# Layer-one norm weights applied to the activations, and weight segments split in halves of 1024 columns

## The chip, the cores and the metric

One core of one Trainium2 chip runs the whole program. The metric is device time in microseconds (us) of one launch. Engines are named as in the profile: PE is TensorE's matmuls and PEld its weight loads, DVE is VectorE, ACT is ScalarE, POOL is GpSimd, SP the queue that issues most transfers.

## The reference, cut to what matters

The input is 512 tokens by 1024 features, all float32. Layer one is a Mamba-2 mixer, layer two a differential attention. Only layer one is touched:

```python
h = rms_norm(x, norm_g)                      # x * rsqrt(mean(x*x) + eps) * norm_g
zxbcdt = h @ w_in                            # 1024 -> 2048 (z) + 4096 (x, B, C) + 32 (dt)
...                                          # conv, SiLU, chunked state-space scan -> y
u = y * silu(z);  u = group_rms_norm(u)      # 8 groups of 256
x = x + (u * gate_norm_g) @ w_out            # 2048 -> 1024
```

`norm_g` has one weight for each row of `w_in`, and `gate_norm_g` one for each row of `w_out`. So each may multiply the rows of the weights or the features of the activation: the product is the same.

## The kernel before, in words

**Three matmuls for one.** Every float32 operand of a big product is cut into two: `hi`, its rounding to the type fp32r, and `lo`, the remainder. `mm3` then adds three matmuls: hi by hi, and the two mixed ones. Making the pair costs one ACT instruction (the rounding copy into `hi`) and one DVE instruction (`lo` = operand minus `hi`).

**Segments.** Layer one's weights come in 32 segments of 1 MB, each a tile `raw` of 128 partitions by 4 blocks (k) of 512 columns: 8 for z, 16 for the eight groups' B, C and x, 8 for the out projection. `order_a` is their order. A segment feeds 16 calls of `mm3`, 48 matmuls. `load` issues the transfer and returns `split`, which gives four pieces, one for each k; a piece is `head` (ACT, `raw` to `whi`) and `rest` (DVE, `raw` and `whi` to `wlo`). With `gains`, both multiply by a norm weight held per partition in `prm`, while they split. `raw`, `whi` and `wlo` have two buffers each: the split of a segment waits until the matmuls of the segment two before it are through, its transfer until the split of the segment two before it is done.

**Who fixes the order.** TensorE's order is the written order (`T.on`). `TURNS` interleaves a segment's blocks for some projections. On DVE and ACT the planner orders layer one's instructions, from priorities and its own estimate of durations; `fetch` lays the pieces of a segment down at high priority. The state-space work of a group (`ssd`) is put between the dense matmuls at the places in `PLACES`. Only the first segment's pieces, which alternate with `split_x`, are in written order on DVE and ACT.

**The places that the change touches.** `split_x` splits the transposed input into `a_hi` and `a_lo` (tiles of `hh`, `hl`), unscaled. At the end of `ssd`, a group's output is transposed into PSUM (`pyt`) and split into `yh` and `yl`, unscaled. `source` hands out the norm weights. Around them: `z_out` (SiLU of a z block, `zs`, frees a PSUM bank), `conv` (a multiplication by `r_row` and three taps on DVE, tile `xc`, frees a PSUM bank); four banks (`mm`) serve the dense products in turn. The dt projection takes its own scaled weights and the raw input.

Of the kernel before, what the change touches and what calls it, by code (L numbers as in the profile page):

```python
# [9 lines left out]
F32 = mybir.dt.float32  # L10
F32R = mybir.dt.float32r
I32 = mybir.dt.int32
AF = mybir.ActivationFunctionType
ALU = mybir.AluOpType
# [42 lines left out]
C_GA, C_GK, C_GB, C_GG, C_SG, C_DTB, C_AL, C_CB, C_CW = 0, 8, 16, 24, 40, 41, 42, 43, 75  # L57
# [24 lines left out]
def trunk(ctx, tc, x, x_t, par, w_dt, w_in, w_out, w_kvqg, w_bo, d_skip, lam_qk, fin_g, out):  # L82
    nc = tc.nc
    V, A, T = (Ordered(tc, e) for e in (nc.vector, nc.scalar, nc.tensor))
# [14 lines left out]
    def ss_bank(name):  # L99
        turns[0] += 1  # L100
        tag = "mm" if turns[0] % turns[1] >= 3 else "ss"
        return psum.tile([P, 512], F32, tag=tag, name=name, bufs=3 if tag == "ss" else 4)
# [8 lines left out]
    segs = []  # L111
# [4 lines left out]
    prm = const.tile([P, C_CB], F32, name="prm")  # L116
# [8 lines left out]
    def source(seg):  # L125
        kind, a, b = seg
        if kind == "z":
            return w_in[a * 6 + b], [prm[:, C_GA + 4 * b + i:C_GA + 4 * b + i + 1] for i in range(4)]
        if kind == "g":
            return w_in[(a // 2) * 6 + 2 + (a % 2) * 2 + b], [prm[:, C_GA + 4 * b + i:C_GA + 4 * b + i + 1] for i in range(4)]  # L130
        if kind == "o":
            return w_out[a * 2 + b], [prm[:, C_GG + 4 * a + i:C_GG + 4 * a + i + 1] for i in range(4)]
        if kind in "bc":
            return w_bo[a], None
        name = f"v{a}" if kind == "v" else a
        at = C_GK if kind in "vk" else C_GB
        ks = range(4 * b, 4 * b + 4) if kind == "v" else range(8)
        return w_kvqg[BLOCKS.index((name, b))], [prm[:, at + i:at + i + 1] for i in ks]
# [5 lines left out]
    def load(i):  # L144

        seg = segs[i]
        src, gains = source(seg)
        nk = 8 if seg[0] in "kqt" else 4
        w = 2048 // nk
        raw = begun[i] if i in begun else wp.tile([P, nk, w], F32, tag="raw", name=f"raw{i}", bufs=2)  # L150
        fetched[0] += 1

        def split():

            pool, tags = (bp, ("dec", "dec")) if seg == ("o", 3, 1) else (wp, ("whi", "wlo"))
            if pool is bp:
                hi, lo = (pool.tile([P, N_DEC], F32R, tag=tag, name=f"{n}{i}", bufs=2)[:, 0:2048].rearrange("p (k n) -> p k n", k=nk)
                          for n, tag in zip(("whi", "wlo"), tags))
            else:
                hi, lo = (pool.tile([P, nk, w], F32R, tag=tag, name=f"{n}{i}", bufs=2) for n, tag in zip(("whi", "wlo"), tags))  # L160
            ready[seg] = (hi, lo)

            def head(k):
                if gains:
                    A.activation(hi[:, k, :], raw[:, k, :], AF.Copy, scale=gains[k])
                else:
                    A.copy(hi[:, k, :], raw[:, k, :])

            def rest(k):
                if gains:  # L170
                    V.scalar_tensor_tensor(out=lo[:, k, :], in0=raw[:, k, :], scalar=gains[k],
                                           in1=hi[:, k, :].bitcast(F32), op0=ALU.mult, op1=ALU.subtract)
                else:
                    V.tensor_tensor(out=lo[:, k, :], in0=raw[:, k, :], in1=hi[:, k, :].bitcast(F32), op=ALU.subtract)

            return [(head, rest, k) for k in range(nk)]

        if i == 0:

            nc.sync.dma_start(raw[:, 0, :], src[:, 0:w])  # L180
            for n in range(2):
                nc.sync.dma_start(xt[0][:, 0, n * 256:(n + 1) * 256], x_t[:, 0, n * 256:(n + 1) * 256])
            nc.sync.dma_start(raw[:, 1, :], src[:, w:2 * w])
            for n in range(2):
                nc.sync.dma_start(xt[0][:, 1, n * 256:(n + 1) * 256], x_t[:, 1, n * 256:(n + 1) * 256])
            for k in range(2, 4):
                nc.sync.dma_start(raw[:, k, :], src[:, k * w:(k + 1) * w])
                nc.sync.dma_start(xt[1][:, k - 2, :], x_t[:, k, :])

            nxt, (src1, _) = wp.tile([P, nk, w], F32, tag="raw", name="raw1", bufs=2), source(segs[1])  # L190
            begun[1] = nxt
            for i in range(2, 4):
                nc.sync.dma_start(xt[i], x_t[:, 2 * i:2 * i + 2, :])
                nc.sync.dma_start(nxt[:, 2 * i - 4:2 * i - 2, :].rearrange("p k n -> p (k n)"), src1[:, (2 * i - 4) * w:(2 * i - 2) * w])
            nc.sync.dma_start(prc[:], par[:, C_CB:N_PAR])
        elif i not in begun:
            nc.sync.dma_start(raw.rearrange("p k n -> p (k n)"), src)
        return split
# [94 lines left out]
    def root1(ss, vb, k, tag):  # L293

        s, y, c, nv = (small.tile([P, 1], F32, tag=f"{tag}_{i}", name=f"{tag}_{i}", bufs=2) for i in "sycn")
        A.activation(s, ss, AF.Sqrt, scale=k, bias=vb)

        def rest():
            V.tensor_scalar(out=nv, in0=ss, scalar1=-k, scalar2=vb, op0=ALU.mult, op1=ALU.subtract)
            V.reciprocal(y, s)  # L300
            V.tensor_scalar(out=c, in0=y, scalar1=nv, scalar2=y, op0=ALU.mult, op1=ALU.mult)
            V.tensor_scalar(out=y, in0=c, scalar1=3.0, scalar2=y, op0=ALU.add, op1=ALU.mult)
            return y

        return rest
# [55 lines left out]
    def new_h(tag):  # L361
        return [res.tile([P, KD, S], F32R, tag=f"hT_{i}", name=f"{tag}_{i}") for i in ("hi", "lo")]
# [9 lines left out]
    hh, hl = new_h("a")  # L372
# [24 lines left out]
    xt = [bp2.tile([P, 2, S], F32, tag="yl", name=f"xt{i}", bufs=4) for i in range(4)]  # L397

    def split_x(k, n=slice(0, S)):
        A.copy(hh[:, k, n], xt[k // 2][:, k % 2, n])  # L400
        V.tensor_tensor(out=hl[:, k, n], in0=xt[k // 2][:, k % 2, n], in1=hh[:, k, n].bitcast(F32), op=ALU.subtract)


    begin = small.tile([P, 1], F32, name="begin", bufs=1)
# [5 lines left out]
    for k in range(4):  # L410
        lay(first[k])
        for n in (slice(0, 256), slice(256, S)) if k < 2 else (slice(0, S),):
            split_x(k, n)
# [5 lines left out]
    for k in range(4, KD):  # L419
        split_x(k)  # L420
# [202 lines left out]
    def ssd(g):  # L623
# [7 lines left out]
        for c in range(NQ):  # L631
            cs = slice(c * P, (c + 1) * P)
# [10 lines left out]
        for j in range(2):  # L643
# [6 lines left out]
            with tc.issue_after(next_b.ins) if next_b else ExitStack():  # L650
                V.tensor_tensor(out=xdt[:, :, 2 * j:2 * j + 2, :], in0=pv, in1=dt_tok[:, :, h2].unsqueeze(3).to_broadcast([P, NQ, 2, HD]), op=ALU.mult)
                V.tensor_tensor(out=dx[:, :, 2 * j:2 * j + 2, :], in0=pv,
                                in1=dsk[:, h2].unsqueeze(1).unsqueeze(3).to_broadcast([P, NQ, 2, HD]), op=ALU.mult)
# [24 lines left out]
        for q in (1, 0):  # L678
            for c in (2 * q, 2 * q + 1):
                for h in reversed(range(R)):  # L680
                    o = (c % 2) * 256 + h * HD
# [14 lines left out]
        for c in (2, 3):  # L696
            T.matmul(po2[:, (c - 2) * 256:(c - 1) * 256], lhsT=cc[:, c * P:(c + 1) * P], rhs=hsf[:, c - 1], start=True, stop=True)
        V.tensor_tensor(out=tmp[:, 1], in0=po1[:, 256:512].rearrange("p (h e) -> p h e", e=HD),
                        in1=eacs_tok[:, 1, hs].unsqueeze(2).to_broadcast([P, R, HD]), op=ALU.mult)
        V.tensor_tensor(out=tmp[:, 2:4], in0=po2.rearrange("p (c h e) -> p c h e", h=R, e=HD),  # L700
                        in1=eacs_tok[:, 2:4, hs].unsqueeze(3).to_broadcast([P, 2, R, HD]), op=ALU.mult)
# [15 lines left out]
        yh = bp2.tile([P, 2, S], F32R, tag="yh", name=f"yh{g}", bufs=4)  # L717
        yl = bp2.tile([P, 2, S], F32R, tag="yl", name=f"yl{g}", bufs=4)
        pyt = [ss_bank(f"pyt{g}_{j}") for j in range(2)]

        n = 2 if g == G - 1 else NQ
        for j, a in [(j, a) for a in range(0, NQ, n) for j in range(2)]:
            if not j:
                yield f"y{a}"
            for c in range(a, a + n):
                T.transpose(pyt[j][:, c * P:(c + 1) * P], tm[:, c, j * P:(j + 1) * P], ident)
            cs = slice(a * P, (a + n) * P)
            A.copy(yh[:, j, cs], pyt[j][:, cs])
            V.tensor_tensor(out=yl[:, j, cs], in0=pyt[j][:, cs], in1=yh[:, j, cs].bitcast(F32), op=ALU.subtract)
        yT[g] = (yh, yl)  # L730

    T.on = True
# [4 lines left out]
    hh, hl = new_h("b")  # L737
# [284 lines left out]
    def half(t, n):  # L1022
        hs = slice(n * 512, (n + 1) * 512)
        return x_tok[:, t, hs], fg[:, hs], ot[t][:, hs], out[t * P:(t + 1) * P, hs]
# [99 lines left out]
    rest = root1(st[h][8][:, 3:4], vb, 4.0 / P, "o1")  # L1124
# [23 lines left out]
    y, f, o, dst = half(3, 0)  # L1148
# [8 lines left out]
    y, f, o, dst = half(3, 1)  # L1157
# [68 lines left out]
```

## Time and profile before

| | |
|---|---|
| time, three runs | median 708.38 us (708.01 to 709.41) |
| profiled execution | 709.16 us, span 707.4 us |
| PE, PEld | busy 697.1 us (99%), 579.8 us (82%) |
| DVE, ACT, POOL | busy 519.5 us (73%), 426.2 us (60%), 113.4 us (16%) |
| transfers | 70.85 MB, mean 100 GB/s |
| costliest group of DVE | `wlo` from `raw`, `prm`, `whi`: 240 instructions, 148.7 us |
| costliest group of ACT | `whi` from `raw`, `prm`: 240 instructions, 133.6 us |

The span runs from the first to the last instruction; what the profiled execution took beyond it lies around the program. Layer one fills about 0 to 410 us, layer two the rest. Nearly every DVE, ACT and PE instruction is recorded under line 73, a helper, so groups are told apart by tile names: `pz`, `pg`, `po` are the PSUM tiles of the z, group and out projections.

### The profile page before, as it was taken

The numbers are of one execution on the slowest core, as the hardware profiler recorded it, in microseconds if no ns is written. First come the engines' busy times: TensorE is split into PE (matmuls) and PEld (weight loads), VectorE is DVE, ScalarE is ACT, GpSimd is POOL, SyncE is SP. The second block draws the span as 40 slices with busy tenths as digits, with TensorE's granted clock in tenths as the row PEclk, the third lists the DMA queues.
The fourth block names the chain that finished last, engine by engine and source line by source line (L and its number), as shares of the span: only waits on it lengthen the run. The fifth ranks groups of instructions, "written<-read, shape, count | busy, mean of one in ns | idle before, by whom it ended". The sixth has DMA issues, their size and how long they took to land.

```text
span 707.4 us, 10489 instructions
## 1 busy us (share of the span) xinstructions
PE 697.1 (99%) x3838; PEld 579.8 (82%) x3838; DVE 519.5 (73%) x1181; ACT 426.2 (60%) x931; POOL 113.4 (16%) x158
## 2 busy tenths in 40 slices
PE   8999999999999999999999999999999999999996
PEld 7787888887788888888888888888888888888884
DVE  5479975888579669568996846457778657788786
ACT  6748673664653636637636357567777567765556
POOL 0008422402406025041110101000000000000002
PEclk9999999999999999999999999999999999999999
DMA  8643313233033331331122311313112221113003
GB/s 296 253 151 152 120 59 149 91 120 120 38 142 120 100 137 62 111 128 60 60 76 105 120 60 49 136 62 113 67 60 79 86 75 61 68 56 116 31 1 119
DMA packets 13492, 70.85 MB, mean 100 GB/s; under 512 B 1793, under 2 KB 3329, under 8 KB 6017
## 3 DMA queue, kind: packets, MB, share of 16 engines
q1 hardware_dynamic: 13008, 69.90, 27.0%
q8 instruction: 30, 0.49, 0.3%
q10 hardware_dynamic: 432, 0.28, 0.1%
q14 instruction: 22, 0.17, 0.1%
HBM read 68.02 MB, written 2.16 MB: 99 GB/s over the span
## 4 chain that ended last, share of the span: by engine, by line
PE 88%; DVE 4%; DMA 3%; ACT 2%; issue 1%; POOL 1%; SPq 0%; ACTq 0%; POOLq 0%
PE pg L73 23%; PE po L73 16%; PE pt L73 8%; PE pz L73 7%; PE pq L73 6%; PE pk L73 6%; PE pv L73 6%; PE pb L73 3%; DMA raw<-in_w_in 3%; PE sc L73 3%; PE pyd L73 2%; PE pc L73 2%; DVE wlo L73 1%; PE pcb L73 1%; PE psA L73 1%
## 5 line engine op out<-in xcount | busy, mean ns | idle before, releaser
L73 DVE SCALAR_TENSOR_TENSOR wlo<-raw,prm,whi 128x512 fp32r<-128x512 f32 (+1 forms) x240 | 148.7, 669 | 49.2 <-ACT whi L73 47.5
L73 ACT ACTIVATE whi<-raw,prm 128x512 fp32r<-128x512 f32 (+1 forms) x240 | 133.6, 628 | 51.2 <-issue 13.0
L73 PE MATMUL pg<-a_hi,whi 128*128 128x512 f32 x256 | 103.1, 403 | 0.8 <-DVE xc L73 0.4
L73 PE MATMUL pg<-a_hi,wlo 128*128 128x512 f32 x256 | 100.3, 392 | 0.1
L73 PE MATMUL pg<-a_lo,whi 128*128 128x512 f32 x256 | 99.8, 390 | 0.0
L73 DVE SCALAR_TENSOR_TENSOR xc<-pg,prc,xc 128x511 f32<-128x511 f32 (+2 forms) x96 | 69.6, 742 | 6.5 <-ACT xc L73 6.0
L73 PEld LDWEIGHTS pg<-a_hi,wlo 128*128 128x128 f32 x256 | 48.0, 188 | 11.5 <-DVE wlo L73 1.5
L73 PEld LDWEIGHTS pg<-a_hi,whi 128*128 128x128 f32 x256 | 48.1, 188 | 11.2 <-ACT xc L73 0.8
L73 PEld LDWEIGHTS pg<-a_lo,whi 128*128 128x128 f32 x256 | 48.1, 188 | 9.3
L73 PE MATMUL po<-whi,yh 128*128 128x512 f32 x128 | 51.7, 404 | 0.1
L73 PE MATMUL pz<-whi,a_hi 128*128 128x512 f32 x128 | 49.8, 398 | 1.3 <-DVE xc L73 0.7
L73 PE MATMUL po<-whi,yl 128*128 128x512 f32 x128 | 50.1, 391 | 0.0
L73 PE MATMUL po<-wlo,yh 128*128 128x512 f32 x128 | 50.0, 390 | 0.0
L73 PE MATMUL pz<-whi,a_lo 128*128 128x512 f32 x128 | 48.9, 390 | 0.0
L73 PE MATMUL pz<-wlo,a_hi 128*128 128x512 f32 x128 | 48.9, 389 | 0.0
L1031 POOL TENSOR_TENSOR ot<-x_tok,fg 128x512 f32<-128x512 f32 x4 | 5.0, 1284 | 248.9 <-DVE x_tok L73 248.9
L73 ACT ACTIVATE s<-s,mx 128x128 f32<-128x128 f32 (+3 forms) x64 | 35.6, 557 | 10.2 <-DVE mx L73 10.1
L73 DVE CUSTOM_DVE_ANT_0 s<-sc,bias 128x128 f32<-128x128 f32 (+3 forms) x64 | 29.3, 488 | 15.3 <-PE sc L73 14.8
L73 ACT ACTIVATE xc<-pg,prc 128x512 f32<-128x512 f32 x32 | 24.8, 775 | 25.2 <-DVE pg L73 19.6
L656 POOL TENSOR_TENSOR xe<-xdt,tok 128x256 f32<-128x256 f32 x24 | 14.1, 613 | 159.8 <-DVE xdt L73 159.8
L73 ACT ACTIVATE xc<-xc 128x512 f32<-128x512 f32 x32 | 20.0, 629 | 28.0 <-DVE xc L73 24.1
L73 ACT ACT_TABLE_LOAD x23 | 29.5, 1283 | 10.2 <-DVE xc L73 8.7
(238 smaller groups left out, 1629.8 us busy)
## 6 DMA issues: line engine op xcount, KB each, us to landing
raw<-in_w_in SPq DMA_DIRECT2D x22, 1024.0 KB, 4.9
raw<-in_w_kvqg SPq DMA_DIRECT2D x16, 1024.0 KB, 4.8
dec<-acs_d SPq DMA_DIRECT2D x8, 1024.0 KB, 5.4
raw<-in_w_out SPq DMA_DIRECT2D x8, 1024.0 KB, 4.8
raw<-in_w_bo SPq DMA_DIRECT2D x4, 1024.0 KB, 4.8
x_tok<-in_x SPq DMA_DIRECT2D x4, 512.0 KB, 8.9
out<-ot SPq DMA_DIRECT2D x6, 256.0 KB, 2.1
raw<-in_w_in SPq DMA_DIRECT2D x4, 256.0 KB, 5.0
```

The lines of the kernel that those rows point to most:

```text
L73: i = op(*args, **kw)
L656: GP.tensor_tensor(out=xe[:, c], in0=xdt[:, c], in1=toe_tok[:, c, hs].unsqueeze(2).to_broadcast([P, R, HD]), op=ALU.mult)
L1031: GP.tensor_tensor(out=o, in0=y, in1=f, op=ALU.mult)
```

## The change

The norm weights go from the weights' split to the activations' split. Layer one's segments are then split by plain copies and subtractions, and two blocks k go into one instruction (128 by 1024), except in the first two segments (z0) and the last two (o3). Layer two is as it was.

```diff
@@ source(seg): "z", "g" and "o"
-            return w_in[a * 6 + b], [prm[:, C_GA + 4 * b + i:C_GA + 4 * b + i + 1] for i in range(4)]
+            return w_in[a * 6 + b], None
...
@@ split()
+            n = 2 if seg[0] in "zgo" and 1 < segs.index(seg) < segs.index(("o", 3, 0)) else 1
+
             def head(k):
+                ks = slice(k, k + n)
                 if gains:
                     A.activation(hi[:, k, :], raw[:, k, :], AF.Copy, scale=gains[k])
                 else:
-                    A.copy(hi[:, k, :], raw[:, k, :])
+                    A.copy(hi[:, ks, :], raw[:, ks, :])
...
-                    V.tensor_tensor(out=lo[:, k, :], in0=raw[:, k, :], in1=hi[:, k, :].bitcast(F32), op=ALU.subtract)
+                    V.tensor_tensor(out=lo[:, ks, :], in0=raw[:, ks, :], in1=hi[:, ks, :].bitcast(F32), op=ALU.subtract)
...
-            return [(head, rest, k) for k in range(nk)]
+            return [(head, rest, k) for k in range(0, nk, n)]
@@ split_x
-        A.copy(hh[:, k, n], xt[k // 2][:, k % 2, n])
-        V.tensor_tensor(out=hl[:, k, n], in0=xt[k // 2][:, k % 2, n], in1=hh[:, k, n].bitcast(F32), op=ALU.subtract)
+        ga = prm[:, C_GA + k:C_GA + k + 1]
+        A.activation(hh[:, k, n], xt[k // 2][:, k % 2, n], AF.Copy, scale=ga)
+        V.scalar_tensor_tensor(out=hl[:, k, n], in0=xt[k // 2][:, k % 2, n], scalar=ga, in1=hh[:, k, n].bitcast(F32),
+                               op0=ALU.mult, op1=ALU.subtract)
@@ ssd(g), its end
-            A.copy(yh[:, j, cs], pyt[j][:, cs])
-            V.tensor_tensor(out=yl[:, j, cs], in0=pyt[j][:, cs], in1=yh[:, j, cs].bitcast(F32), op=ALU.subtract)
+            gg = prm[:, C_GG + 2 * g + j:C_GG + 2 * g + j + 1]
+            A.activation(yh[:, j, cs], pyt[j][:, cs], AF.Copy, scale=gg)
+            V.scalar_tensor_tensor(out=yl[:, j, cs], in0=pyt[j][:, cs], scalar=gg, in1=yh[:, j, cs].bitcast(F32),
+                                   op0=ALU.mult, op1=ALU.subtract)
```

## Rows read from the trace of the kernel before

**Rows 1.** The page: busy us, share of the span, instructions.
```profile
PE 697.1 (99%) x3838; PEld 579.8 (82%) x3838; DVE 519.5 (73%) x1181; ACT 426.2 (60%) x931; POOL 113.4 (16%) x158
```

**Rows 2.** PE's waits: us in total, times, longest.
```profile
PE pz L73 <- DVE xc L73: 0.7, 1, 0.7
PE pz L73 <- ACT a_hi L73: 0.5, 1, 0.5
PE pg L73 <- DVE xc L73: 0.4, 1, 0.4
PE pg L73 <- ACT zs L73: 0.4, 1, 0.4
```

**Rows 3.** Timeline of PE, 52 to 55 us: start, us, instruction, [idle before <-releaser].
```profile
52.84 0.39 PE L73 MATMUL pg<-a_lo,whi 128*128 128x512 f32 x1
53.06 0.39 PE L73 MATMUL pg<-a_hi,wlo 128*128 128x512 f32 x1
53.88 0.47 PE L73 MATMUL pg<-a_hi,whi 128*128 128x512 f32 x1 [0.43 <-DVE xc L73]
```

**Rows 4.** ACT's groups by shape: count, busy us, mean ns, idle before.
```profile
L73 ACT ACTIVATE whi<-raw,prm 128x512 fp32r<-128x512 f32 x144 | 92.9, 714 | 39.0 <-issue 10.8 <-PE pg L73 9.9 <-DMA raw<-in_w_in 5.4
...
L73 ACT CAST whi<-raw 128x512 fp32r<-128x512 f32 x16 | 8.7, 615 | 1.8 <-PE pk L73 1.4 <-PE pb L73 0.4
...
L73 ACT ACTIVATE sq<-x_tok 128x1024 f32<-128x1024 f32 x4 | 4.3, 1065 | 0.6 <-DMA x_tok<-in_x 0.2
```

**Rows 5.** DVE's groups by shape.
```profile
L73 DVE SCALAR_TENSOR_TENSOR wlo<-raw,prm,whi 128x512 fp32r<-128x512 f32 x144 | 107.8, 794 | 29.1 <-ACT whi L73 27.7 <-PE ps_tt L73 1.1
...
L73 DVE SCALAR_TENSOR_TENSOR xc<-pg,prc,xc 128x511 f32<-128x511 f32 x32 | 23.8, 744 | 6.1 <-ACT xc L73 6.0
...
L73 DVE TENSOR_TENSOR wlo<-raw,whi 128x512 fp32r<-128x512 f32 x16 | 10.5, 686 | 1.3 <-ACT whi L73 1.3
...
L73 DVE TENSOR_TENSOR a_lo<-xt,a_hi 128x256 fp32r<-128x256 f32 x4 | 1.5, 419 | 0.0
```

**Rows 6.** Timeline of ACT and DVE, 12 to 14 us: two plain instructions back to back.
```profile
12.88 1.14 ACT L73 CAST a_hi<-xt 128x512 fp32r<-128x512 f32 x2 [0.66 <-DMA xt<-in_x_t]
...
13.53 1.29 DVE L73 TENSOR_TENSOR a_lo<-xt,a_hi 128x512 fp32r<-128x512 f32 x2 [0.48 <-ACT a_hi L73]
```

**Rows 7.** Timeline of ACT, 24 to 38 us.
```profile
26.27 2.56 ACT L73 ACTIVATE whi<-raw,prm 128x512 fp32r<-128x512 f32 x4 [2.98 <-DMA raw<-in_w_in]
...
30.14 2.30 ACT L73 ACTIVATE zs<-pz,ar_col 128x256 f32<-128x256 f32 x6
32.29 2.59 ACT L73 ACTIVATE whi<-raw,prm 128x512 fp32r<-128x512 f32 x4
...
35.46 0.63 ACT L73 COPY ar_row<-aps_r 128x512 f32<-128x512 f32 x1
```

**Rows 8.** Timeline of DVE, 33 to 54 us.
```profile
36.12 1.19 DVE L73 TENSOR_TENSOR pre<-ps_dt,ar_row 32x128 f32<-32x128 f32 x4 [0.29 <-ACT ar_row L73]
...
46.63 2.74 DVE L73 SCALAR_TENSOR_TENSOR wlo<-raw,prm,whi 128x512 fp32r<-128x512 f32 x4 [1.08 <-PE ps_tt L73]
```

**Rows 9.** Busy time by window: bounds, length, PE, PEld, DVE, ACT, POOL, clock, DMA.
```profile
150.00:164.00 14.00, 13.17 (x66) 10.53 (x65) 13.63 (x22) 9.65 (x17) 1.76 (x3) 1.00 0.21 75
```

**Rows 10.** Timeline of DVE, 140 to 192 us.
```profile
150.37 2.08 DVE L73 SCALAR_TENSOR_TENSOR wlo<-raw,prm,whi 128x512 fp32r<-128x512 f32 x3 [0.90 <-ACT whi L73]
```

**Rows 11.** Timeline of ACT, DVE and PE, 187 to 190 us.
```profile
187.46 2.55 ACT L73 ACTIVATE whi<-raw,prm 128x512 fp32r<-128x512 f32 x4
...
188.29 0.75 DVE L73 SCALAR_TENSOR_TENSOR wlo<-raw,prm,whi 128x512 fp32r<-128x512 f32 x1
...
189.09 0.50 PE L73 MATMUL pg<-a_hi,wlo 128*128 128x512 f32 x1
```

**Rows 12.** Timeline of DVE and PE, 58 to 62 us.
```profile
58.36 2.20 DVE L73 SCALAR_TENSOR_TENSOR wlo<-raw,prm,whi 128x512 fp32r<-128x512 f32 x2
...
59.90 0.39 PE L73 MATMUL pg<-a_hi,wlo 128*128 128x512 f32 x1
```

More of the change, by code (lines that the diff above doesn't have):

```diff
@@ L127, in source @@
         if kind == "z":
-            return w_in[a * 6 + b], [prm[:, C_GA + 4 * b + i:C_GA + 4 * b + i + 1] for i in range(4)]
+            return w_in[a * 6 + b], None
         if kind == "g":
-            return w_in[(a // 2) * 6 + 2 + (a % 2) * 2 + b], [prm[:, C_GA + 4 * b + i:C_GA + 4 * b + i + 1] for i in range(4)]
+            return w_in[(a // 2) * 6 + 2 + (a % 2) * 2 + b], None
         if kind == "o":
-            return w_out[a * 2 + b], [prm[:, C_GG + 4 * a + i:C_GG + 4 * a + i + 1] for i in range(4)]
+            return w_out[a * 2 + b], None
         if kind in "bc":
@@ L166, in head @@
                 else:
-                    A.copy(hi[:, k, :], raw[:, k, :])
+                    A.copy(hi[:, ks, :], raw[:, ks, :])
             def rest(k):
+                ks = slice(k, k + n)
                 if gains:
```

## The prediction

> **What bounds the kernel now.** I read the busy times of the page first. PE is busy 697.1 of 707.4 us; DVE stands at 73% and ACT at 60% [rows 1]. So time saved on DVE or ACT counts only where PE waits for them, and the second view is the list of PE's waits. Four in it can be touched, each once: 0.5 us for ACT's `a_hi` (the first matmul), 0.4 for ACT's `zs`, 0.4 and 0.7 for DVE's `xc` [rows 2]. The timeline shows that these are too small by a fixed amount. A matmul of 512 columns is drawn 0.39 us long, but the next starts 0.22 after it; before the matmul at 53.88 the starts lie 0.82 apart while the row shows 0.43 idle [rows 3]. The loss is 0.82 - 0.22 = 0.60, 0.17 more than the idle time. The four waits are so worth 2.0 + 4 x 0.17 = 2.7 us, 0.4% of the time. That is about the ceiling, since all other saved DVE and ACT time lies beside matmuls. The remaining views are timelines around the four waits and around the first matmul of segments that are split just in time, where a slip under 0.17 shows as no wait at all.
>
> **The change, part by part.** Of the 144 scaled splits of 128x512 [rows 4, 5], 16 belong to layer two and 128 to layer one (32 segments of four). Two segments of z0 and two of o3 keep 512 columns (16 pieces), 28 segments go to two pieces of 1024.
>
> *Prices.* On ACT a scaled 512 takes 0.714 us, a plain one 0.615; the nearest plain row of 1024 columns is the square with accumulation, 1.065 [rows 4]. I take 1.06 (ends: 0.96, should the accumulation cost the 0.10 that a scale costs, and twice 0.615 = 1.23, nothing won by the width). Two plain 512 back to back take 1.14 [rows 6], so they overlap by 0.09; two of 1024 take 1.06 + 0.97 = 2.03, against 2.56 for four scaled ones [rows 7]: 0.53 less for a segment. On DVE the scaled subtraction takes 0.744 where nothing disturbs it (row of `xc`) and 0.794 on average for `wlo`; the plain one 0.686 for 512 columns and 0.419 for 256 [rows 5], so 0.267 more per 256 and 1.22 for 1024. Ends: 1.07 (four times 0.267) and 1.59 (twice 0.794, nothing won). Two plain 512 overlap by 2 x 0.686 - 1.29 = 0.08 [rows 6], so two of 1024 take 2.36 against 2.74 for four scaled ones [rows 8]: 0.38 less. Over 28 segments ACT loses about 15 us of work and DVE 11. Against that, 10 pieces of `split_x` and 18 of `yh`/`yl` become scaled: 28 x 0.10 on ACT and 28 x 0.06 on DVE, 2.8 and 1.7 us, spread over the span; PE works on other matmuls meanwhile. If that cover were gone, each would cost its 0.16.
>
> *What gets later.* The first `hi` of a segment is ready 1.06 - 0.71 = 0.35 later, the first `lo` another 1.22 - 0.75 = 0.47 later, 0.82 in all; the second half of the segment is earlier.
>
> *At 31 us.* ACT splits a segment from its landing at 26.27 for 2.56, loads a table, and only then makes `zs`, which frees the bank for which PE waits [rows 7, 2]. With 2.03 in place of 2.56, `zs` comes 0.53 earlier. PE's loss there is 0.4 + 0.17, so PE gains about 0.5 (ends: 0 and 0.57).
>
> *At 54 us.* `ar_row` at 35.46 sits behind a second split of 2.59 [rows 7], so it comes 0.53 + 0.56 = 1.09 earlier. DVE's own split of that segment starts at 32.29 - 0.53 + 1.06 = 32.82 and ends at 35.18, so `pre` starts at about 35.2 in place of 36.12: 0.9 earlier. From there one chain of small dt instructions leads to the `wlo` at 46.63 [rows 8], which then starts at 46.63 - 0.9 + 0.35 and lasts 2.36 in place of 2.74: it ends 0.93 earlier. The conv taps behind it, for which PE waits at 53.88, follow. Of these 0.93 the 0.5 from 31 us are already counted: another 0.43 (ends: 0, and 0.60, the whole wait).
>
> *At 159 to 164 us.* DVE is busy 13.63 of 14 us [rows 9], PE loses 0.7 + 0.17 at the end [rows 2]. The `wlo` at 150.37 waits 0.90 for `whi` [rows 10]; it would wait 0.35 longer, but its four pieces (2.08 for three, so about 2.77) become 2.36, and two `yl` beside them cost 0.12 more. In an unchanged order that is nothing gained. But DVE has about 1.2 us of idle time ahead of the split, and the multiplications by `r_row` are there to fill it. I take 0.35 gained (ends: 0.8 gained, and 0.6 lost where a multiplication stands behind a 1024 piece). The same sequence returns once, near 336 to 346, with a slip of PE under 0.3: 0.25 gained.
>
> *At 189 us.* This segment is split just in time. ACT starts at 187.46, the first `lo` ends at 188.29 + 0.75 = 189.04 and the matmul that reads it starts at 189.09 [rows 11]. Pieces of 1024 make that 0.8 later. Nothing in front of it on ACT's queue is changed. I take 0.5 lost, as the later pieces no longer slip (ends: 0.8 lost, 0.3 gained if the order lets the split start earlier).
> The Trainium skill speaks against the change here: Perfetto Trace Analysis, Optimizing Scalar/DVE Operations, says that where ScalarE and VectorE are not saturated but hold up another engine, breaking instructions up lets work be finished sooner. By that rule the whole 0.8 falls due at every such place, which is the rival of late first pieces below. The trace agrees at this place, with 0.05 of slack, and not at most others (the `wlo` that ends at 49.37 is used from 53.88 on).
>
> *At 59.9 us.* Two `wlo` take 2.20 beside POOL's work instead of about 1.4, and PE reads the first at 59.90 [rows 12]. One piece of 1024 from the same start ends at 59.6 undisturbed and at 60.6 with the whole disturbance: 0 to 0.7 lost; I take 0.3.
> The Trainium skill, SBUF — State Buffer, Who interferes with whom, has VectorE with two SBUF inputs and GpSimd exclude each other for whole instructions. Then one piece would be held once where two are held twice, and the term would be about 0.1; the trace shows the stretched rows, not which rule stretches them.
>
> *At the head.* `whi` gets 0.1 shorter and `a_hi` 0.1 longer in front of the first matmul: nothing (ends 0.2 either way).
>
> *Sum.* -0.5 - 0.43 - 0.35 - 0.25 + 0.5 + 0.3 = -0.73. The profiled execution took 709.16, the span 707.4 and 1.76 around it; it becomes 708.4. That execution was 0.78 above the median of 708.38, so I expect 707.6 for the median.
>
> **Rivals.**
> *All waits go.* With some 9 us of work less on DVE and 12 on ACT, the bank waits vanish: 0.57 + 0.60 + 0.87, the slips of 0.25 near 345 and 0.3 at 189, about 2.5, giving 705.9. For it: DVE is the one behind two of the four waits and is 97% busy at one of them. Against it: the first `lo` of each segment is later, and the order of DVE and ACT isn't written down.
> *Late first pieces, slower.* One mechanism: where the first piece is ready less than 0.82 before its use, PE waits for the rest. Priced at 0.8 (189 us), 0.7 (59.9), and 0.6 at each of the two places where conv's multiplication stands behind a 1024 piece, that is 2.7; with only the 0.5 at 31 us won, 2.2 slower, 710.6. It decides from the point where the chain at 36 us doesn't move, or where more segments than one are just in time. For it: the 0.05 of slack at 189; against it: most segments have microseconds.
> *Hidden anyway.* PE is 99% busy, and what is won at 31 and 54 us is waited away at the next bank: 708.4. It is also what follows if the planner lays the wide pieces so that the change does nothing for the queue of `zs` and `ar_row`, that is, doesn't do what it says.
>
> **How the numbers follow.** My forecast (0.1 to 1.4 faster, so 707.0 to 708.3) has 0.38, all waits gone 0.33, hidden anyway 0.11, late pieces 0.18. A measurement of this kernel tells a change from none at about 0.2%, 1.4 us: below 707.0 is faster, above 709.8 slower. That gives 0.33 faster, 0.49 same, 0.18 slower. Cases of both signs hold much of the chance: 707.0 to 708.3 is the likeliest one's own range, and the range for 8 in 10 reaches to 705.8 on one side, where the ceiling of 2.7 is nearly spent, and to 710.0 on the other.
>
> **What would show it.** Right: in the list of PE's waits those for `zs` and for `xc` near 54 us are gone or smaller; `ar_row` about 1 us earlier; `whi` of 1024 near 1.06 us and `wlo` near 1.22; the first `lo` near 189 us later than its matmul would have been ready. DVE's busy time falls by about 9 to 12 us, ACT's by 12 to 15. Wrong: a new wait of PE for `wlo` or `xc` in another group, a 1024 piece well over 1.3 us, or POOL's chain ending later.

## The result and the profile after

The changed kernel takes 713.51 us (median of six runs, 712.50 to 714.45), the kernel before 708.40 in the runs beside it. The ratio is 1.0071, interval [1.0061, 1.0082]: 5.1 us slower. The forecast was 707.6 with a range that ended at 710.0, so both the size and the sign were wrong.

The head of the page and its busy times, to be read against [rows 1] (busy us, share of the span, instructions):

```profile
span 712.7 us, 10373 instructions
...
PE 699.3 (98%) x3838; PEld 581.0 (82%) x3838; DVE 506.7 (71%) x1125; ACT 412.9 (58%) x875; POOL 113.4 (16%) x158
```

DVE is busy 12.8 us less (9 to 12 were foretold), ACT 13.3 us less (12 to 15), and the span is 5.3 us longer. The prices held too. These are ACT's and DVE's groups of 1024 columns (busy us, mean ns of one, idle before), beside [rows 4, 5]:

```profile
L73 ACT CAST whi<-raw 128x1024 fp32r<-128x1024 f32 x56 | 55.9, 1048 | 36.2 <-PE pg L73 12.7 <-issue 10.5 <-PE po L73 5.7
```

```profile
L73 DVE TENSOR_TENSOR wlo<-raw,whi 128x1024 fp32r<-128x1024 f32 x56 | 70.2, 1284 | 35.2 <-ACT whi L73 35.2
```

I had taken 1.06 and 1.22; undisturbed pieces of DVE do take 1.22. So the work got cheaper and the kernel slower, and the list of PE's waits (us in total, times, longest) says where to look, beside [rows 2]:

```profile
PE pz L73 <- DVE xc L73: 2.9, 1, 2.9
PE pg L73 <- DVE wlo L73: 1.8, 3, 0.9
...
PE aps_r L73 <- POOL adiag L343: 0.5, 1, 0.5
PE pz L73 <- ACT a_hi L73: 0.2, 1, 0.2
```

The waits for `zs` and for `xc` at 54 us have left the list. The one for `xc` in z2 grew from 0.7 to 2.9, three waits for `wlo` are new, and one for POOL's `adiag`.

TensorE's order is written by hand, so the 3838 matmuls of both traces pair off one to one (in the first segment, before 21 us, 17 of them stand in places that are exchanged). I subtracted their start times. The difference, PE's lateness, stays level for long stretches and changes at few places; the table has what it changes by at each, from one level stretch to the next:

| before, at us | change in us | what PE waits for in the changed kernel |
|---|---|---|
| up to 27 | -0.06 | |
| 27.7 | +0.71 | POOL's `adiag` |
| 31.0 | -0.48 | `zs`, earlier |
| 53.9 | -0.71 | `xc`, earlier |
| 60.6 | -0.16 | nothing listed |
| 66.7 | +0.22 | nothing listed (the matmuls that read `xc`) |
| 84.4 | +0.42 | nothing listed (the matmuls that read `xc`) |
| 140 | +1.02 | `wlo`, second segment of g3 |
| 159.5 | -0.38 | nothing: a slip of the kernel before is gone |
| 163.2 | +2.18 | `xc`, in the second segment of z2 |
| 164 to 166 | +1.60 | nothing: the same matmuls run slower |
| 188 to 192 | +0.41 | `wlo`, first segment of g4 |
| 326.6 | +0.73 | `wlo`, second segment of g7 |
| 345.7, 349.6 | -0.38, +0.38 | nothing listed |
| after 400 | -0.21 | nothing listed, in small steps |

They add up to 5.3, and the last matmul starts 5.3 later. Some two thirds, 3.4 us, fall between 159 and 166 us: 3.78 lost at the wait and behind it, 0.38 won just ahead of it. Here is DVE's timeline there in the changed kernel (start, us, instruction, count):

```profile
151.66 2.36 DVE L73 TENSOR_TENSOR wlo<-raw,whi 128x1024 fp32r<-128x1024 f32 x2 [3.04 <-ACT whi L73]
153.94 0.69 DVE L73 TENSOR_TENSOR pg<-pg,ar_row 128x512 f32<-128x512 f32 x1
...
162.72 0.74 DVE L73 SCALAR_TENSOR_TENSOR xc<-pg,prc,xc 128x511 f32<-128x511 f32 x1
163.38 0.69 DVE L73 TENSOR_TENSOR pg<-pg,ar_row 128x512 f32<-128x512 f32 x1
163.97 1.22 DVE L73 TENSOR_TENSOR wlo<-raw,whi 128x1024 fp32r<-128x1024 f32 x1
165.10 0.75 DVE L73 SCALAR_TENSOR_TENSOR xc<-pg,prc,xc 128x509 f32<-128x509 f32 x1
165.76 1.22 DVE L73 TENSOR_TENSOR wlo<-raw,whi 128x1024 fp32r<-128x1024 f32 x1
```

And the same in the kernel before (its first split there is in [rows 10]):

```profile
152.37 0.69 DVE L73 TENSOR_TENSOR pg<-pg,ar_row 128x512 f32<-128x512 f32 x1
...
161.69 1.40 DVE L73 SCALAR_TENSOR_TENSOR xc<-pg,prc,xc 128x511 f32<-128x511 f32 x2
163.00 0.69 DVE L73 TENSOR_TENSOR pg<-pg,ar_row 128x512 f32<-128x512 f32 x1
163.60 2.73 DVE L73 SCALAR_TENSOR_TENSOR wlo<-raw,prm,whi 128x512 fp32r<-128x512 f32 x4
```

The instruction to watch is a conv tap, the `xc` of 509 columns. It is the last reader of the PSUM bank that PE's second block of z2 writes. Before, it is the second of the two `xc` at 161.69: it ends 1.40 later, at 163.09, and PE starts at 163.24. After, two instructions that used to follow it stand ahead of it, the multiplication at 163.38 and one `wlo` of 1024 columns at 163.97. It ends at 165.85, and PE starts at 166.00. Of the 2.76 us between the two, 1.03 were there before DVE reached the first of these taps (162.72 against 161.69), and 1.73 are the two instructions that moved in front.

The first delay is in the main not made here. The first multiplication by `r_row` starts at 153.94 in place of 152.37, 1.57 later. Of these, 0.96 are PE's lateness from the places before: ACT's part of the first split waits for PE to be through with an older segment. ACT before:

```profile
149.62 2.57 ACT L73 ACTIVATE whi<-raw,prm 128x512 fp32r<-128x512 f32 x4 [0.80 <-PE pg L73]
```

and after:

```profile
150.58 2.00 ACT L73 CAST whi<-raw 128x1024 fp32r<-128x1024 f32 x2 [2.49 <-PE pg L73]
```

The wider first `whi` adds 0.33 (DVE's split starts 1.29 later), and the two wide `wlo` in front of the multiplication, in place of three narrow ones, 0.28. DVE stood idle for 3.04 us ahead of its split, and none of the multiplications was laid there. PE itself comes to the wait 0.58 late, so of the 2.76 it loses 2.18 here.

The second cost at this place is on no list of waits. PE's timeline around the wait, after:

```profile
162.71 0.39 PE L73 MATMUL pz<-whi,a_lo 128*128 128x512 f32 x1
166.00 0.47 PE L73 MATMUL pz<-whi,a_hi 128*128 128x512 f32 x1 [2.90 <-DVE xc L73]
...
166.58 0.63 PE L73 MATMUL pz<-whi,a_lo 128*128 128x512 f32 x1
167.01 1.91 PE L73 MATMUL psA<-xe,bt 128*128 128x256 f32 x4
```

and the same wait and the same four `psA` before:

```profile
163.24 0.47 PE L73 MATMUL pz<-whi,a_hi 128*128 128x512 f32 x1 [0.72 <-DVE xc L73]
...
164.01 1.02 PE L73 MATMUL psA<-xe,bt 128*128 128x256 f32 x4
```

Four matmuls take 1.91 in place of 1.02. The busy times by window (bounds, length, PE, PEld, DVE, ACT, POOL, granted clock, DMA) show why:

```profile
164.00:166.00 2.00, 0.00 (x1) 0.04 (x1) 2.00 (x4) 0.83 (x2) 0.04 (x1) 1.00 0.00 0
166.00:168.00 2.00, 2.00 (x6) 1.60 (x7) 2.00 (x3) 0.58 (x1) 0.00 (x0) 0.62 0.12 12
168.00:170.00 2.00, 2.00 (x13) 1.17 (x13) 1.61 (x3) 1.00 (x2) 0.59 (x1) 0.53 0.78 246
170.00:172.00 2.00, 2.00 (x65) 1.93 (x62) 1.46 (x3) 0.00 (x0) 0.64 (x2) 1.00 0.65 270
```

After 2.9 us without a matmul the granted clock is 0.62 and 0.53 for about 4 us, that is, mostly the lower of its levels, 1.2 GHz in place of 2.4. Before, it is 1.00 throughout, after a wait of 0.72 us.

The late first pieces, on the timelines of ACT, DVE and PE, after (the lines from 191.12 on answer to [rows 11]):

```profile
135.17 0.42 ACT L73 ACTIVATE tmp<-dx 128x256 f32<-128x256 f32 x1 [0.56 <-DVE dx L73]
...
138.83 1.97 ACT L73 CAST whi<-raw 128x1024 fp32r<-128x1024 f32 x2
...
139.89 1.23 DVE L73 TENSOR_TENSOR wlo<-raw,whi 128x1024 fp32r<-128x1024 f32 x1 [1.25 <-ACT whi L73]
...
141.17 0.51 PE L73 MATMUL pg<-a_hi,wlo 128*128 128x512 f32 x1 [0.52 <-DVE wlo L73]
...
191.12 1.99 ACT L73 CAST whi<-raw 128x1024 fp32r<-128x1024 f32 x2
...
192.74 1.23 DVE L73 TENSOR_TENSOR wlo<-raw,whi 128x1024 fp32r<-128x1024 f32 x1
...
194.01 0.50 PE L73 MATMUL pg<-a_hi,wlo 128*128 128x512 f32 x1 [0.91 <-DVE wlo L73]
```

and ACT before, at the first of the two places:

```profile
137.91 2.55 ACT L73 ACTIVATE whi<-raw,prm 128x512 fp32r<-128x512 f32 x4
140.36 0.40 ACT L73 ACTIVATE tmp<-dx 128x256 f32<-128x256 f32 x1
```

In both places the wide first `wlo` ends just as the matmul that reads it starts (139.89 + 1.23 = 141.12, and 141.17). At the first it ends 1.72 later than before (its piece there ran from 138.65 for 0.75, to 139.40). The width explains 0.80. The other 0.92 is order again, on ACT this time: an instruction that stood behind the split, the `tmp` at 140.36, now stands ahead of it (135.17, with the reading of its sum, 0.18, behind it), and the split starts at 138.83 in place of 137.91. The place at 327 us has the same exchange. The exchange alone makes no wait: the kernels below that keep narrow pieces here have it too, PE's list shows no wait there, and it loses at most 0.25 in them.

### The profile page after: what moved, and what is told of

It is laid out like the page before. It is cut to its first block, busy times and chain, and to the rows that moved or that the text cites. A ratio compares the mean times of both kernels' runs of the same rounds, so it can differ in the third digit from the quotient of the medians.

```text
span 712.7 us, 10373 instructions
## 1 busy us (share of the span) xinstructions
PE 699.3 (98%) x3838; PEld 581.0 (82%) x3838; DVE 506.7 (71%) x1125; ACT 412.9 (58%) x875; POOL 113.4 (16%) x158
## 3 DMA queue, kind: packets, MB, share of 16 engines
HBM read 68.02 MB, written 2.16 MB: 98 GB/s over the span
## 4 chain that ended last, share of the span: by engine, by line
PE 84%; DVE 5%; DMA 4%; issue 2%; ACT 2%; POOL 2%; SPq 0%; ACTq 0%; POOLq 0%
PE pg L73 19%; PE po L73 16%; PE pt L73 7%; PE pz L73 7%; PE pq L73 6%; PE pk L73 6%; PE pv L73 6%; PE pb L73 3%; PE sc L73 3%; PE pyd L73 2%; PE pc L73 2%; DMA dec<-acs_d 1%; DMA x_tok<-in_x 1%; PE psA L73 1%; PE pcb L73 1%
## 5 line engine op out<-in xcount | busy, mean ns | idle before, releaser
L73 DVE TENSOR_TENSOR wlo<-raw,whi 128x1024 fp32r<-128x1024 f32 (+1 forms) x88 | 91.0, 1067 | 39.1 <-ACT whi L73 39.1
L73 ACT CAST whi<-raw 128x1024 fp32r<-128x1024 f32 (+1 forms) x88 | 73.7, 891 | 47.6 <-PE pg L73 12.7
L73 DVE SCALAR_TENSOR_TENSOR wlo<-raw,prm,whi 128x256 fp32r<-128x256 f32 (+1 forms) x112 | 52.0, 519 | 21.1 <-ACT whi L73 20.7
L73 PEld LDWEIGHTS pg<-a_hi,wlo 128*128 128x128 f32 x256 | 48.1, 188 | 13.3 <-DVE wlo L73 3.1
L73 ACT ACTIVATE whi<-raw,prm 128x256 fp32r<-128x256 f32 (+1 forms) x112 | 51.2, 530 | 13.1 <-PE pk L73 6.1
```

The lines of the kernel that those rows point to most:

```text
L73: i = op(*args, **kw)
```

## The experiments

**The theory** after the result: the order that the planner lays on DVE at z2 costs some 3.5 us (a wait and a lower clock behind it), late first pieces in three segments a little over 2, and the move of the norm weights alone is a gain. **The rival**: wide instructions hurt in themselves, by holding up DVE, POOL or PE wherever they stand. A second rival was that the scaled splits of the activations cost what is lost. All diffs are against the changed kernel.

### Norm weights moved, all pieces of 512

```diff
-            n = 2 if seg[0] in "zgo" and 1 < segs.index(seg) < segs.index(("o", 3, 0)) else 1
+            n = 1
```

> The change with every piece at 512 columns: only the norm weights are moved. Theory (order): the loss comes from where the planner puts DVE's wide wlo pieces of z2, ahead of the last conv tap that frees a bank for PE near 163 us, and from wide first pieces in just-in-time segments. In this kernel the tap stands ahead of all four wlo pieces again, so PE's wait there is at most 0.9 us, no slow stretch of PE follows, and the time is 706.8 to 708.2. Rival (scale): the scaled splits of the activations (yh, yl, a_hi, a_lo) are the loss; then the time stays at 712 to 714.

Measured: 707.30 us, ratio to the kernel before 0.9989 [0.9979, 0.9998]. Its list of PE's waits is one line long, a wait for a constant at the start:

```profile
PE warm L73 <- POOL ident masks.py:199: 1.5, 1, 1.5
```

So the move of the weights is worth 1.05 us, and the whole loss comes with the width. The second rival falls. PE's gains at 31 and 54 us are here too (0.46 and 0.71): the plain copy suffices for what I had put down to the width. At 159.5 and 163 us PE gains 0.23 and 0.66, both slips of the kernel before.

### Only the two segments of z2 at 512, and only these two at 1024

```diff
-            n = 2 if seg[0] in "zgo" and 1 < ...
+            n = 2 if seg[0] in "zgo" and seg[:2] != ("z", 2) and 1 < ...
```

> The change with only the two segments of z2 at 512 columns. Theory (order): PE's wait of 2.9 us near 163 us falls to under 1 us and its slow stretch after it goes: 713.5 - 1.9 - 1.5 = about 710 us; the three waits for wlo (near 141, 194 and 332 us in the changed kernel) stay. Rival (wide pieces are late everywhere): only a share of two segments in 28 comes back, 713.

Measured: 710.25 us, 1.0026 [1.0015, 1.0037]. The wait for `xc` is gone and the clock stays at 1.00. It is 1.9 us above the kernel before, the changed one 5.1: the two segments are worth 3.2.

```diff
+            n = 2 if seg[:2] == ("z", 2) else 1
```

> The kernel with only the norm weights moved (707.3 us), in which two segments of 32, those of z2, go back to 1024 columns. Theory (order): the planner puts a wide wlo piece of z2's second segment ahead of the tap again, PE waits some 3 us near 163 us and runs at a lower granted clock behind it: 707.3 + 1.9 + 1.5 = about 710.7 us, more than half of the whole loss from two segments. Rival (wide pieces are late everywhere): two segments in 28 cost a fourteenth of the loss, 707.5 to 708.

Measured: 710.86 us, 1.0033 [1.0015, 1.0052]. That is 2.16 above the kernel before where all narrow is 1.05 below it, each by the runs of the kernel before on its own chip, so the two segments alone cost 3.2 again, with 8 of the change's 112 wide instructions. This speaks for the place and against the width as such. There is no late first piece ahead of it here: PE comes to the place 0.93 us earlier than in the kernel before, and loses 2.43 at the wait all the same. The wait is 2.9 us, and the clock is down behind it:

```profile
166.00:168.00 2.00, 2.00 (x6) 1.58 (x5) 2.00 (x4) 0.15 (x1) 0.00 (x0) 0.50 0.66 188
```

### The width on one engine at a time

```diff
-                    V.tensor_tensor(out=lo[:, ks, :], in0=raw[:, ks, :], in1=hi[:, ks, :].bitcast(F32), op=ALU.subtract)
+                    for kk in range(k, k + n):
+                        V.tensor_tensor(out=lo[:, kk, :], in0=raw[:, kk, :], in1=hi[:, kk, :].bitcast(F32), op=ALU.subtract)
```

> The change with ACT's copies at 1024 columns and DVE's subtractions at 512. Theory (order): here the planner puts all four wlo pieces of z2's second segment ahead of the tap, 4 x 0.6 us in place of one piece of 1.13, so PE's wait near 163 us grows to about 4 us and the time is 713.5 to 715.5, although no DVE instruction is wide. Rival (wide DVE instructions block the queue): no wide DVE instruction, so the loss is gone, 707 to 709.

Measured: 713.95 us, 1.0078 [1.0063, 1.0093]: as slow as the change, with every DVE piece narrow. PE's waits, and DVE's timeline at the place:

```profile
PE pz L73 <- DVE xc L73: 4.3, 1, 4.3
...
PE po L73 <- DVE xc L73: 1.0, 1, 1.0
```

```profile
162.32 2.50 DVE L73 TENSOR_TENSOR wlo<-raw,whi 128x512 fp32r<-128x512 f32 x4
164.73 3.38 DVE L73 SCALAR_TENSOR_TENSOR xc<-pg,prc,xc 128x509 f32<-128x509 f32 x5
```

Here all four narrow `wlo` stand ahead of the tap, and the wait is 4.3. The rival falls for DVE: the order does it, not a wide instruction there. The copies on ACT are wide here; the kernel below with the tap put ahead keeps them so and changes the order. No wait for `wlo` is listed in this kernel.

```diff
-                    A.copy(hi[:, ks, :], raw[:, ks, :])
+                    for kk in range(k, k + n):
+                        A.copy(hi[:, kk, :], raw[:, kk, :])
```

> The change with DVE's subtractions at 1024 columns and ACT's copies at 512. Theory (order): the tap stands ahead of the wlo pieces of z2's second segment, as in the kernel before, so PE's wait near 163 us is under 1.2 us and no slow stretch follows; the waits for wlo in just-in-time segments stay at about half a microsecond each: 708.5 to 710. Rival (wide DVE instructions block the queue): 712 to 714.

Measured: 710.09 us, 1.0025 [1.0015, 1.0035]. The planner kept the tap ahead of both wide `wlo`, and the longest wait for `xc` is 0.7. What is lost here is mostly the late first pieces: PE loses 1.13 at 140 us and 0.94 at 327, both at a `wlo`. I had expected 708.5 to 710, just too low.

### The wide pieces kept, the tap put ahead of them

The four pieces (two on each engine) of the second z2 segment are laid only when the last tap of conv on that bank has been issued.

```diff
+            if seg == ("z", 2, 1):
+                held.extend(pieces_)
+                continue
...
+        if j == 2:
+            with tc.issue_after(conv_end[27].ins), tc.high_priority():
+                for piece in held:
+                    lay(piece)
```

> The changed kernel with all its wide pieces; only the two wlo pieces of z2's second segment are held behind the last tap of the c convolution on DVE. Theory (order): the tap comes one wide piece (1.13 us) earlier, PE's wait near 163 us falls from 2.9 to about 1.8 us, and the time to 712.4, or to 711 if PE's clock stays up after the shorter wait. Rival (width itself, wherever it stands): the wide pieces only change places, 713 to 714.

Measured: 710.94 us, 1.0030 [1.0020, 1.0039]: 2.2 us above the kernel before, where the change is 5.1 above. DVE, PE, and the window behind the wait:

```profile
164.14 0.73 DVE L73 SCALAR_TENSOR_TENSOR xc<-pg,prc,xc 128x509 f32<-128x509 f32 x1
164.80 2.35 DVE L73 TENSOR_TENSOR wlo<-raw,whi 128x1024 fp32r<-128x1024 f32 x2
...
165.02 0.47 PE L73 MATMUL pz<-whi,a_hi 128*128 128x512 f32 x1 [1.76 <-DVE xc L73]
```

```profile
166.00:168.00 2.00, 2.00 (x34) 1.59 (x34) 2.00 (x4) 0.37 (x1) 0.62 (x1) 1.00 0.00 0
```

With the tap ahead, the tap ends 0.98 sooner, the wait is 1.8 and no longer 2.9, and behind 1.8 us the clock stays at 1.00. So 2.9 of the 5.1 us went, with every piece as wide as in the change. I had expected 712.4, or 711 if the clock stays up: the second came.

### The wait kept, PE given something to do in it

24 matmuls on a constant fill the wait; their product goes into a spare bank and is used by nothing.

```diff
+                if j == 2 and t == 1:
+                    fill_ps = long_bank("filler")
+                    for _ in range(24):
+                        T.transpose(fill_ps[:, 0:P], ident, ident)
```

> The changed kernel with 24 transposes of the identity on PE (0.108 us each by the starts of such transposes, about 2.6 us) in the place where PE waits 2.9 us near 163 us; DVE's order is the same. Theory: the wait costs twice, 1.9 us more idle time and, because PE stood idle, about 1.5 us of matmuls at the lower clock behind it. The filler lies inside the wait and keeps PE busy: the granted clock stays at 1.00 from 164 to 172 us and the time falls to about 712. Rival: the slow stretch comes from what DVE and POOL do there; 713 to 714, clock as low as before.

Measured: 712.24 us, 1.0046 [1.0028, 1.0063]. PE's timeline:

```profile
162.48 2.78 PE L73 MATMUL filler<-ident 128*128 128x128 f32 x24
165.53 0.47 PE L73 MATMUL pz<-whi,a_hi 128*128 128x512 f32 x1 [0.27 <-DVE xc L73]
...
166.29 1.02 PE L73 MATMUL psA<-xe,bt 128*128 128x256 f32 x4
```

The next block's first matmul still starts 3.3 us after the last of the block before it, yet the clock is 1.00 from 160 to 172 us and `psA` takes 1.02 again. Useless work won 1.6 us (5.1 against 712.24 - 708.70 = 3.5). The interval just meets that of the change, [1.0061, 1.0082], so by the times alone this is not certain; the trace says the same, for PE loses 2.17 at the wait as in the change, and 0.02 behind it in place of 1.60.

### The late first pieces, and both cures together

```diff
-            n = 2 if seg[0] in "zgo" and 1 < ...
+            n = 2 if seg[0] in "zgo" and seg not in (("g", 3, 1), ("g", 4, 0), ("g", 7, 1)) and 1 < ...
```

> The changed kernel with only the three segments at 512 columns whose first wlo piece PE waits for (the second of g3, the first of g4, the second of g7); z2 stays wide. Theory: late first pieces and the order near 163 us are two causes that add up. The three waits cost 0.7 + 0.6 + 0.4 = 1.7 us against the kernel before, so the time falls from 713.5 to about 711.8, and PE's wait of about 3 us near 163 us stays. Rival (one cause: the three waits are an echo of the late state near 163 us): two of the three stay and the time is 713.

Measured: 711.55 us, 1.0038 [1.0026, 1.0051]. That is 2.7 above the kernel before in place of 5.1: the three segments are worth 2.4. No wait for `wlo` is left in its list, and that for `xc` is still 2.9.

The Trainium skill, Perfetto Trace Analysis, Optimizing Scalar/DVE Operations, says that breaking instructions up may let work be done sooner where engines that aren't saturated hold up another. These three segments agree, with 2.4 us for six wide pieces on each engine. The kernel with width on ACT alone shows that breaking DVE's up is not enough by itself: PE waited 4.3 us in it.

```diff
+            n = 2 if seg[0] in "zgo" and seg[:2] != ("z", 2) and seg not in (("g", 3, 1), ("g", 4, 0), ("g", 7, 1)) and 1 < ...
```

> The changed kernel with 512 columns in z2's two segments and in the three that PE waits for (the second of g3, the first of g4, the second of g7); 23 segments stay wide. Theory (order and just-in-time pieces): all of PE's waits for wlo near 141, 194 and 332 us go, about 2 us less than with z2 narrow alone: 708 to 709; what is left over the narrow kernel is the late start near 28 us, where POOL's adiag waits. Rival (wide pieces are late everywhere): other segments become the late ones, 709.5 to 710.5.

Measured: 707.47 us, 0.9985 [0.9976, 0.9994], with 23 of 28 segments still wide. It beats the change by some 6 us and the kernel before by 1.2. No wait of PE is left but the two at the kernel's start, for a constant and `a_hi`. It came out below the 708 to 709 expected: `adiag` was not late in its profile. The loss of 0.42 near 84 us is still there.

```diff
+            n = 2 if ... and seg not in (("g", 0, 0), ("g", 3, 1), ("g", 4, 0), ("g", 7, 1)) and 1 < ...
```

> Wide pieces where they did no harm: z2, the three just-in-time segments and the first segment of g0 at 512 columns, 22 segments at 1024. Theory: no wait of PE is left in layer one but the first matmul's, so the time is that of the kernel with only the norm weights moved, 706.8 to 707.6: wide pieces bring nothing, since DVE and ACT hold up PE nowhere. Rival (the 9 us of DVE work saved by wide pieces count): 705 to 706.

Measured: 707.16 us, 0.9981 [0.9972, 0.9990]. The intervals of this one, of the last and of all narrow overlap. So the width, where it does no harm, is worth nothing that could be measured.

## Why the prediction was wrong

*Prices*: right. 1.05 and 1.22 measured for 1.06 and 1.22 taken; pairs of 2.00 and 2.36 for 2.03 and 2.36.

*At 31 us* (-0.5) and *At 54 us* (-0.43): right in mechanism and near in size (-0.48 and -0.71, the second beyond its end of 0.60; -0.46 and -0.71 with all pieces narrow), but not by the width, as the narrow kernel shows. In the profiled execution of the change a loss of 0.71 at 27.7 us eats the first; I had not looked at `adiag` (below).

***At 159 to 164 us* (-0.35) is the step that failed.** It was worked out "in an unchanged order", with DVE's idle time to be filled by the multiplications by `r_row`. The order changed, as it did on ACT near 140 us. DVE's idle time ahead of the split grew from 0.90 to 3.04 us and nothing was put into it. Both pieces of the first split were laid ahead of the first multiplication, and a multiplication and one piece of the second split ahead of the tap that frees PE's bank. I had seen the first danger and bounded it at 0.6 lost ("where a multiplication stands behind a 1024 piece"). The second, a bank-freeing tap behind the piece, I had not: the planner could put any of the instructions that were ready there ahead, and the bound should have held the whole 1.2 of a piece and the 0.6 of a multiplication. Measured: 1.80 lost between 159 and 164 us (2.18 at the wait, less the 0.38 just ahead of it). The gain that I forecast here was to be had, 0.89, with narrow pieces.

The clock behind the wait was in no bound. I priced a wait as idle time plus 0.17, from a row with 0.43 of idle time; this wait cost another 1.60. The filler shows that it came from PE's being idle, and with the pinned order, behind 1.8 us, it did not come.

*The repeat near 336 to 346* (-0.25): PE gains 0.38 there in the change and gives it back 4 us later, and the same with z2 and the three segments narrow; with all pieces narrow it gains 0.23 and keeps it.

*At 189 us* (+0.5): right, 0.41. (With all pieces narrow PE gains 0.82 there, so against that the wide pieces cost 1.2.) But I took it for the only segment split just in time. Two more, near 140 and 327 us, lost 1.02 and 0.73. Before, they showed no wait: near 140 the first `lo` was ready at 139.40 and read at 140.35, 0.95 to spare. The 0.82 of the width alone would have fitted in; with the 0.92 of ACT's new order it did not. I had not asked each segment for its spare time, nor for what could come ahead of its split.

*At 59.9 us* (+0.3): wrong sign, -0.16 in the profiled execution, where the piece took 1.53; it isn't a width's gain, for all narrow has the same -0.16. The term has a tail on the other side, told below.

*The rivals.* "Late first pieces, slower" named the sign and gave 710.6. Its condition, more just-in-time segments than one, was met, and a multiplication did stand behind a wide piece; but it had 0.6 for a place that cost 3.4, since it missed the tap and the clock. "All waits go" describes the kernel with norm weights moved and nothing widened: its waits went, and it gained 1.05 of the 2.5 I gave for that. I had not asked what each half of the change does alone; the half that gains was cheap to separate.

A term that I had at nothing is the 0.42 near 84 us. There an ACT `xc` that PE reads stands behind a pair of wide `whi`, where before it stood ahead of the split. Every profiled kernel with wide copies on ACT there loses 0.40 to 0.42, and the three with narrow copies there lose nothing, the one with width on DVE alone among them: an exchange of order again, and it comes with ACT's width.

## What to carry to other kernels

Where a planner orders an engine's queue, a change of an instruction's length is a change of order: list what could be laid ahead of each instruction that frees a bank for PE, and bound the loss by the whole of it. Ask every segment how long before its use its first piece is ready, not only those that show a wait. And look at the granted clock behind every new wait of PE: the slower matmuls there stand in no list of waits.

## What the runs showed of the hardware

**The clock behind a wait.** In the profiles around 163 us, waits of 0.7 and 1.8 us were followed by a granted clock of 1.00, and waits of 2.9 us (three kernels) and 4.3 us by stretches of about 3 to 7 us near 0.5. The kernel with z2 alone wide ran ten times, with mean granted clocks from 0.992 to 0.999. The three runs at 0.998 or 0.999 took least (709.85 to 709.91 us), so the fall seems not to follow the wait each time; only one of the ten was profiled, at 0.992.

**DVE and POOL on SBUF.** `adiag` is four POOL instructions of 0.40 us each, 1.47 together before. In the changed kernel they meet a wide `wlo`. POOL's and DVE's timelines, after:

```profile
25.75 2.45 POOL L343 TENSOR_TENSOR adiag<-ident,ar_col 128x128 f32<-128x128 f32 x4 [3.37 <-DVE ar_col L73]
...
26.67 2.61 DVE L73 TENSOR_TENSOR wlo<-raw,whi 128x1024 fp32r<-128x1024 f32 x2 [1.07 <-ACT whi L73]
```

One of the four took 1.38, some 1.0 more, and the `wlo` pair 0.25 more than its 2.36. Of the seven kernels profiled with this piece wide, three show it (2.45, 2.46 and 3.44 us, begun at 25.61 to 25.86); in the other four `adiag` begins at 25.35 or earlier and takes 1.47 or 1.48. It isn't the width's alone: with this segment at 512, in the last kernel above, `adiag` took 1.92.

The largest case came by chance, in the profiled execution of the last kernel above, which took 712.93 us where its median is 707.16. Its timelines of DVE, POOL and PE:

```profile
58.95 8.11 DVE L73 TENSOR_TENSOR wlo<-raw,whi 128x1024 fp32r<-128x1024 f32 x1
...
59.56 4.07 POOL L621 TENSOR_TENSOR dec<-dec,tok 128x512 f32<-128x512 f32 x4
63.59 2.39 POOL L622 TENSOR_SCALAR_AFFINE_SELECT dec<-dec 128x512 f32<-128x512 f32 x4
...
70.07 0.91 PE L73 MATMUL pxt<-ident,xc 128*128 128x128 f32 x4 [4.46 <-ACT xc L73]
```

One piece of 1.22 us stood for 8.11, and ended 1.08 after POOL's run of eight instructions: it looks held for the whole run, and PE lost 4.5 us to it and more to the clock (0.58 and 0.57 from 70 to 74 us). In the other profiles a piece of this segment, of either width, was never over 2.02 us. The Trainium skill, SBUF — State Buffer, Who interferes with whom, says that a DVE instruction with two SBUF inputs contends with a GpSimd instruction that reads SBUF, and that the order of issue decides who is held. Both cases agree with the first, with 1.38 in place of 0.40 and 8.11 in place of 1.22. As to the order, the `adiag` that took 1.38 began at 26.83, after the `wlo` at 26.67; in the second case the `wlo` (58.95) and a POOL instruction (58.96) began too close together to tell. My reading of it in the prediction, that one piece is held once, does not fit the second case: here one piece stood through eight. Whether the width makes this likelier was not tried.
